# Attention: weights times v in six products of 256 columns per block instead of four of 512, and some subtractions moved from VectorE to GpSimd

## The chip, the cores and the metric

The kernel runs on one core of one Trainium2 chip. The metric is device time in microseconds. Before the change three runs gave 906.5, 906.73 and 907.61 us; the median is 906.73. A profile of one further execution (907.17 us) is used for all readings. The engines are named as in the profile: PE is TensorE (PEld its weight loads), DVE is VectorE, ACT is ScalarE, POOL is GpSimd, SP is SyncE, which only issues transfers.

## The reference

One layer of a hybrid block for 1024 tokens of width 1024: a modulated RMSNorm, one input projection, two branches (sliding-window attention and a recurrent branch), their output projections, a merge, an output product, the residual and a last norm. What matters here is the attention:

```python
WINDOW = 128
BLOCK = 128
...
kb = jnp.concatenate([kp[:, :-1], kp[:, 1:]], axis=2)
vb = jnp.concatenate([vp[:, :-1], vp[:, 1:]], axis=2)
s = jnp.einsum('bnqkgd,bnskd->bnkgqs', qb, kb) * (1.0 / math.sqrt(hd))
...
band = (diff >= 0) & (diff < WINDOW)
s = jnp.where(mask[None, :, None, None], s, -1e30)
m = jnp.maximum(jnp.max(s, axis=-1, keepdims=True), sink)
p = jnp.exp(s - m)
denom = jnp.sum(p, axis=-1, keepdims=True) + jnp.exp(sink - m)
o = jnp.einsum('bnkgqs,bnskd->bnqkgd', p / denom, vb)
```

There are 16 query heads in four groups that share a key and value head (head width 64), and 8 blocks of 128 queries. As window and block are both 128, a query sees exactly 128 keys: those of its own block up to itself, and those of the block before that come after its own place. The recurrent branch ends in `y_rnn @ w_rnn_proj`, a full product of 1024 x 1024 by 1024, which also matters below.

## The kernel before, in words

**Precision.** Every product is made of parts: an operand is split into a rounded high part and the rest as a low part (names ending in `h` and `l`), and three of the four products of parts are summed. The high part is a cast on ACT (`cast`, line 105), the low part a subtraction on DVE (`rest`, line 111).

**Stages.** The input projection (line 709) runs to about 557 us, then the attention stage to about 735 us, then the attention's projection, the merge and the output product (line 1863). From the input projection to the end of the attention, the order of each engine's instructions is the order in which the program writes them; a scheduler orders the last stage.

**The attention stage.** It is a loop of 35 iterations over 32 units u: unit u is group g = u // 8 and block n = u % 8, with four heads. It is pipelined: iteration u makes the scores of unit u (line 1330, eight products of 256 columns; `s_ps`), the exponentials of unit u - 1 (ACT, line 1355), the transposed weights of unit u - 2 (line 1369, `pt`) and the product with v of unit u - 3 (line 1403, `pv`). To keep TensorE busy, one or two pieces of *filler* stand between them (`piece`): slots of the input projection that were kept back, then pieces of the recurrent branch's output product (line 173, names `yh`, `yl`, `wh`, `wl`, output `rp`), twelve products of 512 columns each. On TensorE an iteration reads: transposes of u - 2, product of u - 3, scores of u + 1, filler.

**What a unit's scores go through.** ACT copies the scores of the own block (line 1339), DVE puts those of the block before in the places k > q (line 1345, `copy_predicated`, the last reader of `s_ps`, of which there is one buffer), takes the maximum (1350), ACT the exponential, DVE the reciprocal of the sum (1361) and the division (1362). So the 128 weights of a query lie in one row of 128 places k, own block for k <= q, block before for k > q.

**The product with v.** TensorE transposes the four heads' weights into `pt` (keys down, 4 x 128 queries across). ACT rounds it to `phc` (1374), DVE takes the rest, `plc` (1380), and GpSimd makes two masked copies, `phm` and `plm`, in which places k > q are zero (`masks`, line 1389). With v of the block before as if all places were its own, and the difference of the two blocks' v for the masked places, the output is

```python
prods = [(vd[:, n % 2, 1 if n else 0, :], m) for m in full]
prods += [(vd[:, n % 2, 0, :], m) for m in masked]
```

four products of 512 columns, into one PSUM tile `pv`. The stationary side holds v's high part in 64 columns and its low part in the other 64, so each product gives both. ACT and DVE join the two halves (1412, 1413, 1423, 1424) into `yq`. A block with n = 0 has no block before: two products, no masks.

**vd.** `v_prep` (line 1154 on) makes v and its differences for each group early in the program and stores them with two transfers to `vd_d` in DRAM, on GpSimd's queue. `load_v` (1305) loads 256 KB for two neighbouring units, on the same queue, two iterations ahead. The loads of keys and queries, of the recurrent weights (`r`) and of the recurrent branch's outputs (`yh`, `yl`, `load_y`) go through SP's queue. `load_y` is called at the first recurrent pieces, and each `yh` or `yl` of 512 KB is read by the products of its eighth kc.

**Around it.** The gate of the attention is applied in every second iteration by DVE (1538, both operands in SBUF), then ACT rounds (1543) and DVE subtracts (1548, both operands in SBUF) in the next. The filler's weights are split by `prep_r`: the cast is put off to the end of an iteration (`later_a`), the subtraction on DVE to the next iteration, behind the maximum (`later_d`). Two of four recurrent pieces bring one such pair each.

**GpSimd in an iteration:** a copy of the sinks into the place of the 129th weight (1318), the two masks, every second iteration the load of vd.

Of the kernel before, what the change touches and what calls it, by code (L numbers as in the profile page):

```python
# [50 lines left out]
BANKS = (0, 1, 2, 3), (4, 5, 6, 7)  # L51


@with_exitstack
def tile_hybrid_block(ctx, tc, x, pk, rows, posr, posi, c_row, w_ss, w_gate, w_main, w_v,
# [53 lines left out]
    def rest(dst, src, scale=1.0):  # L109
        if scale == 1.0:  # L110
            V.tensor_tensor(out=dst[1][:], in0=src, in1=f32(dst[0][:]), op=ALU.subtract)  # L111
# [18 lines left out]
    vd_d = [tc.dram_tile([P, 8, 2, P], F32, name=f"vd_d{g}") for g in range(NG)]  # L130
# [1023 lines left out]
    def v_prep(g):  # L1154
# [19 lines left out]
        def f3():  # L1174
# [3 lines left out]
            dma(vd_d[g][:, 1:8, 1, :], t["vs"][:, 0:7, :], G)  # L1178
            dma(vd_d[g][:, :, 0, :], t["dv"][:], G)
# [102 lines left out]
    def open_attn():  # L1282
# [9 lines left out]
        load_v(0)  # L1292

# [11 lines left out]
    def load_v(m):  # L1305
        g, n0 = m // 4, (m % 4) * 2
        vd = at.tile([P, 2, 2, P], F32R, tag="vd", name="vd", bufs=2)
        if n0:
            dma(vd[:], vd_d[g][:, n0:n0 + 2, :, :], G)
        else:  # L1310
            dma(vd[:, 0, 0, :], vd_d[g][:, 0, 0, :], G)
            dma(vd[:, 1, :, :], vd_d[g][:, 1, :, :], G)
        U["v", m] = vd
# [51 lines left out]
    def transposed(u):  # L1365
        px = U.pop(("s", u))[1]
        pt = psx.tile([P, 4, P], F32, tag="t", name="pt")
        for j in range(4):
            W["pe"] = T.transpose(pt[:, j, :], px[:, j, 0:P], ident[:])  # L1369
        U["t", u] = [pt]  # L1370

    def split_a(u):
        phc = at.tile([P, 4, P], F32R, tag="phc", name="phc")
        A.copy(phc[:], U["t", u][0][:])
        U["t", u].append(phc)

    def split_d(u):
        pt, phc = U.pop(("t", u))
        plc = at.tile([P, 4, P], F32R, tag="plc", name="plc")
        V.tensor_tensor(out=plc[:], in0=pt[:], in1=f32(phc[:]), op=ALU.subtract)  # L1380
        U["m", u] = phc, plc

    def masks(u):
        phc, plc = U["m", u]
        ms = []
        if u % 8:
            for s_, tag in ((phc, "phm"), (plc, "plm")):
                d_ = W["yo"].tile([P, 4, P], F32R, tag=tag, name=tag)
                G.affine_select(out=d_[:], in_=f32(s_[:]), pattern=[[0, 4], [1, P]],
                                compare_op=ALU.is_ge, fill=0.0, base=0,  # L1390
                                channel_multiplier=-1)
                ms.append(d_)
        U["m", u] = [phc, plc], ms

    def values(u):
        n = u % 8
        vd = U["v", u // 2]
        full, masked = U.pop(("m", u))
        prods = [(vd[:, n % 2, 1 if n else 0, :], m) for m in full]
        prods += [(vd[:, n % 2, 0, :], m) for m in masked]  # L1400
        pv = psx.tile([P, 4 * P], F32, tag="v", name="pv")
        for i, (b, m) in enumerate(prods):
            W["pe"] = T.matmul(pv[:], b, m[:].rearrange("p j q -> p (j q)"),  # L1403
                               start=(i == 0), stop=(i == len(prods) - 1))
        U["pv", u] = [pv[:].rearrange("p (a e q) -> p a e q", a=2, e=2)]
        if n % 2 == 0 and u // 2 + 1 < 16:
            load_v(u // 2 + 1)

    def join_a(u):
        pvv = U["pv", u][0]  # L1410
        ob = W["yo"].tile([P, 2, P], F32, tag="ob", name="ob")
        A.copy(ob[0:64], pvv[64:128, :, 0, :])
        A.copy(ob[64:128], pvv[0:64, :, 1, :])
        U["pv", u].append(ob)

    def join_d(u):
# [5 lines left out]
        yo = W["yq"][:, :, (n % 2) * P:(n % 2 + 1) * P]  # L1422
        V.tensor_tensor(out=yo[0:64], in0=pvv[0:64, :, 0, :], in1=ob[0:64], op=ALU.add)
        V.tensor_tensor(out=yo[64:128], in0=pvv[64:128, :, 1, :], in1=ob[64:128], op=ALU.add)
# [12 lines left out]
    def prep_r(e, i):  # L1437
# [4 lines left out]
        later_d.append(lambda: rest(O[e, i], R[e][i]))  # L1442
# [617 lines left out]
```

## Time and profile before

| | |
|---|---|
| median of three runs | 906.73 us (906.5 to 907.61) |
| profiled execution | 907.17 us, of it 905.5 us span from the first to the last instruction |
| TensorE busy | 895.4 us, 99% of the span, clock 0.999 of full speed |
| VectorE, ScalarE, GpSimd busy | 717.1, 567.4, 124.7 us |
| DMA | 180.74 MB, 200 GB/s over the span |

Lines of the profile give an engine, an operation, what it writes and reads, its shape, a count and a duration. The duration of a product is modelled and overlaps with the next one's, so the distance between starts is what a product costs TensorE. "idle before <-X" is time in which the engine waited for X. For a transfer the profile gives the issue, and the time from there to its landing.

### The profile page before, as it was taken

How to read it: one execution, taken by the hardware profiler on the slowest of the kernel's cores; microseconds unless marked ns; L12 is line 12 of the kernel's file. 1: busy time of each engine (PE TensorE's matmuls, PEld its weight loads, DVE VectorE, ACT ScalarE, POOL GpSimd, SP SyncE). 2: the span in 40 equal slices, each digit the busy share in tenths (PEclk: the TensorE clock that was granted, in tenths of full speed). 3: DMA queues.
4: the chain of work that ended last, by engine and by line, in shares of the span. 5: the costliest groups of instructions: out<-in, count | busy, mean ns of one | idle time of the engine just before them, and what ended most of it. 6: DMA issues, size and time to landing. Idle time of an engine off the chain costs nothing.

```text
span 905.5 us, 12654 instructions
## 1 busy us (share of the span) xinstructions
PE 895.4 (99%) x4258; PEld 746.2 (82%) x4259; DVE 717.1 (79%) x1073; ACT 567.4 (63%) x1098; POOL 124.7 (14%) x216
## 2 busy tenths in 40 slices
PE   9999999999999999999999999999999999999997
PEld 6789888888888888888888888888888888888886
DVE  6987688988669875987788597999989846578855
ACT  7965554654566855786485884888888732115535
POOL 6520251200000000000000002343443300000000
PEclk9999999999999999999999999999999999999999
DMA  9829489772435353354446367996655289416604
GB/s 355 339 69 286 164 258 319 256 235 95 151 128 180 123 209 135 125 183 162 157 144 213 105 201 242 344 401 217 214 202 203 83 306 367 140 47 232 209 1 186
DMA packets 87349, 180.74 MB, mean 200 GB/s; under 512 B 8642, under 2 KB 29138, under 8 KB 87284
## 3 DMA queue, kind: packets, MB, share of 16 engines
q1 hardware_dynamic: 83200, 167.07, 52.5%
q0 software_dynamic: 3936, 12.59, 4.4%
q8 instruction: 34, 0.56, 0.3%
q14 instruction: 31, 0.25, 0.1%
q10 hardware_dynamic: 148, 0.27, 0.1%
HBM read 121.34 MB, written 58.95 MB: 199 GB/s over the span
## 4 chain that ended last, share of the span: by engine, by line
PE 52%; issue 42%; DVE 3%; ACT 2%; DMA 1%; POOL 0%; DVEq 0%; ACTq 0%; POOLq 0%
PE rp L173 14%; PE bk L709 10%; PE out L1863 6%; PE pmain L173 5%; PE s_ps L1330 3%; PE pv L1403 3%; PE pmain L485 2%; PE bk L485 2%; PE pt L1369 1%; DMA yl_d<-it 1%; PE pmain L1579 1%; PE pmain L1580 1%; PE pmain L1578 1%; ACT jk L1881 1%; PE bk L256 1%
## 5 line engine op out<-in xcount | busy, mean ns | idle before, releaser
L709 PE MATMUL bk<-nh,wh 128*128 128x512 f32 x368 | 143.4, 390 | 0.0
L709 PE MATMUL bk<-nl,wh 128*128 128x512 f32 x368 | 143.3, 389 | 0.0
L709 PE MATMUL bk<-nh,wl 128*128 128x512 f32 x368 | 98.4, 389 | 0.0
L111 DVE TENSOR_TENSOR wl<-r,wh 128x512 fp32r<-128x512 f32 x109 | 74.8, 692 | 23.3 <-ACT wh L105 23.2
L105 ACT CAST wh<-r 128x512 fp32r<-128x512 f32 x107 | 65.6, 618 | 32.1 <-PE rp L173 11.8
L709 PEld LDWEIGHTS bk<-nh,wl 128*128 128x128 f32 x368 | 69.1, 188 | 14.3
L709 PEld LDWEIGHTS bk<-nh,wh 128*128 128x128 f32 x368 | 69.2, 188 | 14.2
L709 PEld LDWEIGHTS bk<-nl,wh 128*128 128x128 f32 x368 | 69.1, 188 | 14.1
L709 PE MATMUL bk<-hh,wh 128*128 128x512 f32 x184 | 71.7, 390 | 0.0
L709 PE MATMUL bk<-hl,wh 128*128 128x512 f32 x184 | 71.6, 389 | 0.0
L111 DVE TENSOR_TENSOR wl<-ws,wh 128x512 fp32r<-128x512 f32 x76 | 52.1, 686 | 7.2 <-ACT wh L105 7.1
L62 POOL DMA_DIRECT2D yh_d<-av x1 | 0.6, 567 | 371.9 <-ACT av L1092 371.9
L1355 ACT ACTIVATE p<-p,small 128x129 f32<-128x129 f32 x128 | 50.0, 396 | 0.0
L709 PE MATMUL bk<-hh,wl 128*128 128x512 f32 x184 | 49.2, 389 | 0.0
L105 ACT CAST wh<-ws 128x512 fp32r<-128x512 f32 x76 | 46.0, 614 | 4.8 <-DVE ws L731 2.4
L709 PEld LDWEIGHTS bk<-hh,wl 128*128 128x128 f32 x184 | 34.6, 188 | 7.1
L709 PEld LDWEIGHTS bk<-hh,wh 128*128 128x128 f32 x184 | 34.6, 188 | 7.1
L709 PEld LDWEIGHTS bk<-hl,wh 128*128 128x128 f32 x184 | 34.6, 188 | 7.1
L1330 PEld LDWEIGHTS s_ps<-ks,qs 128*128 128x128 f32 x256 | 34.1, 189 | 4.4 <-DVE p L1345 2.0
L1330 PE MATMUL s_ps<-ks,qs 128*128 128x256 f32 (+1 forms) x256 | 35.6, 282 | 0.3 <-DVE p L1345 0.2
L709 PE MATMUL bk<-hha,wh 128*128 128x512 f32 x92 | 35.8, 390 | 0.0
L709 PE MATMUL bk<-hla,wh 128*128 128x512 f32 x92 | 35.8, 389 | 0.0
(378 smaller groups left out, 2293.1 us busy)
## 6 DMA issues: line engine op xcount, KB each, us to landing
r<-w_main SPq DMA_DIRECT2D x100, 256.0 KB, 4.2
wada<-w_ss SPq DMA_DIRECT2D x16, 512.0 KB, 9.0
qs<-q_d SPq DMA_DIRECT2D x16, 512.0 KB, 5.2
wo_d<-wr SPq DMA_DIRECT2D x28, 256.0 KB, 3.1
wo<-wo_d SPq DMA_DIRECT2D x14, 512.0 KB, 5.6
ks<-k_d SPq DMA_DIRECT2D x12, 384.0 KB, 4.3
xt<-x SPq DMA_DIRECT2D x8, 512.0 KB, 7.1
sma_d<-c SPq DMA_DIRECT2D x16, 256.0 KB, 4.4
```

The source lines that it names most:

```text
L105: A.copy(dst[0][:], src)
L111: V.tensor_tensor(out=dst[1][:], in0=src, in1=f32(dst[0][:]), op=ALU.subtract)
L173: mm = T.matmul(ps[hf], ww, xx[kc][hf], start=(kc == 0 and ww is w_h and xx is xh), stop=(kc == KC - 1 and xx is xl))
L256: T.matmul(bk[i % 2], zero[:, 0:P], zero, start=True, stop=True)
L485: T.matmul(starts[c][hf], ww[:, c0:c0 + P], xh[kc][hf], start=(kc == 0 and t_ == "h"), stop=(kc == KC - 1 and t_ == "l"))
L709: W["pe"] = T.matmul(ps, ww[:, kc * P:(kc + 1) * P], b[kc][i], start=(first and n == 0), stop=(n == 11), skip_group_check=not first)
L1330: W["pe"] = T.matmul(o, qs[:, j, qc], ks[:, kb:n % 2 + 2, b, :], start=(b == 0), stop=(b == 1))
L1355: A.activation(px[:, j, :], px[:, j, :], AF.Exp, bias=sm[:, 0, j:j + 1], accum_out=sm[:, 1, j:j + 1])
L1369: W["pe"] = T.transpose(pt[:, j, :], px[:, j, 0:P], ident[:])
L1403: W["pe"] = T.matmul(pv[:], b, m[:].rearrange("p j q -> p (j q)"), start=(i == 0), stop=(i == len(prods) - 1))
L1578: T.matmul(o, hh[kc][th][:, ts_], wh[:, cols], start=(kc == 0), stop=False)
L1863: T.matmul(o, a[k][x_][:, p * P:(p + 1) * P], b[k][y_][:, cols], start=(first and k == 0 and i == 0), stop=(k == 3 and i == 2), skip_group ...
```

## The change

The columns of the product with v are regrouped: the 128 queries of a block are taken in two halves l of 64, so that 4 heads x 64 queries make 256 columns. For the lower half, places 64 to 127 always belong to the block before, so only places 0 to 63 need the mask; for the upper half places 0 to 63 always belong to the own block, and only 64 to 127 need it. So the masked high and the masked low part of a half each fill only 64 partitions, and both go into one tile `pm` of 128 partitions, against a stationary side that holds the difference twice. Each half has three products of 256 columns (`phc`, `plc`, `pm`). `vd` now holds, for each unit and each half, its own base and its own doubled difference.

What goes with it:
- `v_prep` stores eight transfers for each group instead of two, and `vd_d` is twice as large.
- `load_v` loads 256 KB for each unit instead of for two (64 KB where n = 0), with three buffers.
- The transposes write two pieces of 64 columns; the joins read four-dimensional views.
- `masks` makes four selects of 64 x 256 instead of two of 128 x 512; two of them read one half of the partitions and write the other.
- In the attention stage the filler's low parts are subtracted by GpSimd, at the end of the iteration, right behind the cast; VectorE has 18 subtractions fewer.

The diff's core:

```diff
-    def rest(dst, src, scale=1.0):
+    def rest(dst, src, scale=1.0, eng=V):
         if scale == 1.0:
-            V.tensor_tensor(out=dst[1][:], in0=src, in1=f32(dst[0][:]), op=ALU.subtract)
+            eng.tensor_tensor(out=dst[1][:], in0=src, in1=f32(dst[0][:]), op=ALU.subtract)
...
-            dma(vd_d[g][:, 1:8, 1, :], t["vs"][:, 0:7, :], G)
-            dma(vd_d[g][:, :, 0, :], t["dv"][:], G)
+            o, vs, dv = vd_d[g], t["vs"], t["dv"]
+            dma(o[:, 1:8, 0, 0, :], vs[:, 0:7, :], G)
+            dma(o[:, 0, 0, 0, :], vs[:, 0, :], G)
+            dma(o[TOP, 1:8, 1, 0, :], vs[TOP, 1:8, :], G)
+            dma(o[END, 1:8, 1, 0, :], vs[END, 0:7, :], G)
+            for l, half_ in enumerate((TOP, END)):
+                for to in (TOP, END):
+                    dma(o[to, 1:8, l, 1, :], dv[half_, 1:8, :], G)
...
-    def load_v(m):
-        g, n0 = m // 4, (m % 4) * 2
-        vd = at.tile([P, 2, 2, P], F32R, tag="vd", name="vd", bufs=2)
-        if n0:
-            dma(vd[:], vd_d[g][:, n0:n0 + 2, :, :], G)
+    def load_v(u):
+        g, n = u // 8, u % 8
+        vd = U["v", u] = at.tile([P, 2, 2, P], F32R, tag="vd", name="vd", bufs=3)
+        if n:
+            dma(vd[:], vd_d[g][:, n, :, :, :], G)
...
-            for s_, tag in ((phc, "phm"), (plc, "plm")):
-                d_ = W["yo"].tile([P, 4, P], F32R, tag=tag, name=tag)
-                G.affine_select(out=d_[:], in_=f32(s_[:]), pattern=[[0, 4], [1, P]],
+            pm = W["yo"].tile([P, HALF], F32R, tag="pm", name="pm")
+            lo, hi = slice(0, 256), slice(256, HALF)
+            for to, s_, from_, cols in ((TOP, phc, TOP, lo), (END, phc, END, hi),
+                                        (END, plc, TOP, lo), (TOP, plc, END, hi)):
+                G.affine_select(out=pm[to, cols], in_=f32(s_[from_, cols]),
+                                pattern=[[0, 4], [1, 64]], compare_op=ALU.is_ge, fill=0.0,
...
-        for i, (b, m) in enumerate(prods):
-            W["pe"] = T.matmul(pv[:], b, m[:].rearrange("p j q -> p (j q)"),
-                               start=(i == 0), stop=(i == len(prods) - 1))
-        if n % 2 == 0 and u // 2 + 1 < 16:
-            load_v(u // 2 + 1)
+        for l in range(2 if n else 1):
+            cols = slice(l * 256, l * 256 + 256) if n else slice(0, HALF)
+            for i, t_ in enumerate(m):
+                W["pe"] = T.matmul(pv[:, cols], vd[:, l, i // 2, :], t_[:, cols],
+                                   start=(i == 0), stop=(i == len(m) - 1))
+        if u + 2 < 32:
+            load_v(u + 2)
...
-        later_d.append(lambda: rest(O[e, i], R[e][i]))
+        later_d.append(lambda: rest(O[e, i], R[e][i], eng=G if "att" in W else V))
...
-        do_later(later_d)
         low = [steps_[2] for steps_ in high]
...
-        do_later(later_a)
+        do_later()
```

How the instructions stand now. TensorE, the transposes of one unit, the product with v of the unit before and the scores that follow; before:

```order
L1369 MATMUL pt<-ident,p 128x128 x4
L1403 MATMUL pv<-phc,vd 128x512
L1403 MATMUL pv<-plc,vd 128x512
L1403 MATMUL pv<-phm,vd 128x512
L1403 MATMUL pv<-plm,vd 128x512
L1330 MATMUL s_ps<-ks,qs 128x256 x8
```

The same place on TensorE now:

```order
L1375 MATMUL pt<-ident,p 128x2x64 x4
L1409 MATMUL pv<-phc,vd 128x256
L1409 MATMUL pv<-plc,vd 128x256
L1409 MATMUL pv<-pm,vd 128x256
L1409 MATMUL pv<-phc,vd 128x256
L1409 MATMUL pv<-plc,vd 128x256
L1409 MATMUL pv<-pm,vd 128x256
L1336 MATMUL s_ps<-ks,qs 128x256 x8
```

Four products became six of half the width; nothing else on TensorE changed its place in the whole program.

GpSimd, two iterations near unit 6, before (the sinks' copy, the masks, the select of a first block's scores, loads of vd):

```order
L62 DMA vd<-vd_d_85 128x512
L1318 COPY p<-pk_t 128x4
L1389 AFFINE_SELECT phm<-phc 128x512
L1389 AFFINE_SELECT plm<-plc 128x512
L1348 AFFINE_SELECT p<-p 128x4x128
L1318 COPY p<-pk_t 128x4
L1389 AFFINE_SELECT phm<-phc 128x512
L1389 AFFINE_SELECT plm<-plc 128x512
L62 DMA vd<-vd_d_86 128x128
```

The same two iterations on GpSimd now:

```order
L63 DMA vd<-vd_d_85 128x512
L1324 COPY p<-pk_t 128x4
L1396 AFFINE_SELECT pm<-phc 64x256 x2
L1396 AFFINE_SELECT pm<-plc 64x256 x2
L112 TENSOR_TENSOR wl<-r,wh 128x512
L1354 AFFINE_SELECT p<-p 128x4x128
L63 DMA vd<-vd_d_85 128x512
L1324 COPY p<-pk_t 128x4
L1396 AFFINE_SELECT pm<-phc 64x256 x2
L1396 AFFINE_SELECT pm<-plc 64x256 x2
L112 TENSOR_TENSOR wl<-r,wh 128x512
L63 DMA vd<-vd_d_86 128x128
```

The subtraction stands behind the masks and ahead of the next load of vd, and there is a load in each iteration. VectorE at the same place, one iteration before:

```order
L1548 TENSOR_TENSOR al<-yq,ah 128x2x256
L1345 COPY_PREDICATED p<-mgt,s_ps 128x4x128
L1350 TENSOR_REDUCE small<-p 128x4
L111 TENSOR_TENSOR wl<-r,wh 128x512
L1361 RECIPROCAL small<-small 128x4
L1362 TENSOR_TENSOR p<-p,small 128x4x128
```

and now:

```order
L1554 TENSOR_TENSOR al<-yq,ah 128x2x256
L1351 COPY_PREDICATED p<-mgt,s_ps 128x4x128
L1356 TENSOR_REDUCE small<-p 128x4
L1367 RECIPROCAL small<-small 128x4
L1368 TENSOR_TENSOR p<-p,small 128x4x128
```

Only the subtraction left; line 1548 (1554 now) keeps its place ahead of line 1345 (1351), and a subtraction on GpSimd falls in that stretch of the iteration. In the last stage, which the scheduler orders, a few loads on SP and a few casts and subtractions on ACT and DVE change places among themselves.

More of the change, by code (lines that the diff above doesn't have):

```diff
@@ L1378, in split_d @@
         pt, phc = U.pop(("t", u))
[L1379 to L1380 removed]
+        plc = at.tile([P, HALF], F32R, tag="plc", name="plc")
+        V.tensor_tensor(out=plc[:], in0=pt, in1=f32(phc[:]), op=ALU.subtract)
         U["m", u] = phc, plc
```

45 lines of the change are left out of this document (20 added, 25 removed).

## The prediction

> **What bounds the kernel now.** I read the page's shares first, then the table of stretches (engine busy time, granted clock, DMA share), then the timelines of the attention stage, and last who waited for whom.
>
> ```profile
> PE 895.4 (99%) x4258; PEld 746.2 (82%) x4259; DVE 717.1 (79%) x1073; ACT 567.4 (63%) x1098; POOL 124.7 (14%) x216
> ...
> 570.00:616.50 46.50, 46.41 (x261) 39.56 (x260) 43.27 (x79) 39.17 (x124) 19.13 (x36) 1.00 1.01 381
> 616.50:735.00 118.50, 118.50 (x637) 100.64 (x636) 103.89 (x195) 93.66 (x289) 42.33 (x74) 1.00 0.52 178
> 735.00:905.50 170.50, 163.99 (x735) 136.02 (x733) 111.45 (x155) 61.97 (x109) 0.00 (x0) 0.99 0.50 184
> ```
>
> The columns after a stretch are its length, then PE, PEld, DVE, ACT and POOL busy, the clock, the DMA share and GB/s. TensorE is busy throughout and at full clock, so a microsecond taken off its stream is a microsecond off the end, as long as nothing else becomes late. The attention stage (about 557 to 735 us) is where something can: VectorE is busy 93% in the first of its two stretches, and there the DMA engines are full, with a share of 1.01 at 381 GB/s. From 616.5 us on the DMAs have half of their time free.
>
> **The change part by part.** *The products.* One iteration of the attention loop on TensorE, up to the next one's transposes, then two neighbours of the 256-column products that make v, which load new weights for each product, and the count of the masked products:
>
> ```profile
> 644.08 0.60 PE L1369 MATMUL pt<-ident,p 128*128 128x128 f32 x4
> 644.44 0.48 PE L1403 MATMUL pv<-phc,vd 128*128 128x512 f32 x1
> 644.75 0.39 PE L1403 MATMUL pv<-plc,vd 128*128 128x512 f32 x1
> 644.99 0.40 PE L1403 MATMUL pv<-phm,vd 128*128 128x512 f32 x1
> 645.22 0.39 PE L1403 MATMUL pv<-plm,vd 128*128 128x512 f32 x1
> 645.45 1.11 PE L1330 MATMUL s_ps<-ks,qs 128*128 128x256 f32 x8
> 646.40 0.40 PE L173 MATMUL rp<-hha,wh 128*128 128x512 f32 x1
> ...
> 649.15 0.60 PE L1369 MATMUL pt<-ident,p 128*128 128x128 f32 x4
> ...
> 75.00 0.28 PE L1578 MATMUL pmain<-wh,hha 128*128 128x256 f32 x1
> 75.12 0.28 PE L1579 MATMUL pmain<-wl,hha 128*128 128x256 f32 x1
> ...
> L1403 PE MATMUL pv<-phm,vd x28: 389/397/398, 579.0 to 729.5; 128*128 128x512 f32 x28
> ```
>
> Only starts count here, as the shown durations overlap. The four products hold TensorE from 644.44 to 645.45, 1.01 us: 0.31 to the second start and 0.23 for each of the others, so the first one, behind the transposes, costs 0.08 extra. A 256-column product costs 0.12 us (75.00 to 75.12; the eight of the scores take 0.95, 0.119 each). Six make 6 x 0.12 + 0.08 = 0.80 us. The saving is 0.21 us in each of 28 blocks (the four with n = 0 keep two products of 512): 5.9 us. Taken with 0.119 and no weight load showing it is 0.22, or 6.2 us. I take 28 x 0.215 = 6.0 us. The four transposes stay four of 128 columns, written as two pieces of 64, and the joins of line 1412 to 1424 move the same number of elements; I cost both at nothing. If a piece cost 10 ns more, the joins would still be hidden behind TensorE's filler, and the 128 transposes would cost 1.3 us.
>
> *Loads of vd.* This is the term against the change. Before, one load of 256 KB serves two blocks; now each block with n > 0 loads its own 256 KB, 64 KB for n = 0. The stretch in which this happens is the one with full DMA engines, and it holds the loads of the recurrent branch's y, which the filler products read:
>
> ```profile
> vd<-vd_d POOLq DMA_DIRECT2D x4, 256.0 KB, 6.4
> vd<-vd_d POOLq DMA_DIRECT2D x1, 128.0 KB, 5.3
> vd<-vd_d POOLq DMA_DIRECT2D x1, 64.0 KB, 5.2
> ...
> 606.58 0.32 SPq L62 DMA_DIRECT2D yl<-yl_d  x1
> ...
> yl<-yl_d SPq DMA_DIRECT2D x1, 512.0 KB, 9.9
> ...
> 618.04 0.62 PE L173 MATMUL rp<-yl,wh 128*128 128x512 f32 x2
> ...
> 585.00:590.00 5.00, 5.00 (x30) 4.28 (x29) 4.20 (x8) 4.43 (x15) 2.25 (x5) 1.00 0.95 310
> ```
>
> The last y piece was issued at 606.58 and landed 9.9 us later, at 616.5; its first reader starts at 618.04. That is 1.5 us of slack. The vd loads of 570 to 616 move 4 x 256 + 128 + 64 = 1216 KB before. Afterwards about eight of 256 and one of 64 fall there, 2112 KB: 0.9 MB more, at 381 GB/s 2.4 us of all engines. From 585 to 590 the engines had a share of 0.95, so 0.25 us is free there; and about half of the last load, 0.35 us, comes too late to matter. I take 1.7 us: the piece lands at 618.2. Its reader would be ready at 618.04 less the seven shortened blocks u = 1 to 7 (1.5 us), at 616.5, so TensorE waits 1.7 us there and is then 0.2 us behind the old time. The 21 blocks after it save 21 x 0.215 = 4.5 us. Bounds: no wait at all (6.0 us kept) and the whole 2.4 us (3.7 us kept).
>
> The stores that prepare vd_d go from two to eight on GpSimd's queue for each of four groups. They stand ahead of the next group's load of v there, but that load is asked for six slots ahead and TensorE reads vd_d only in the attention stage; I cost them at nothing. If that cover failed, VectorE would wait some microseconds for v in a stage in which TensorE has its weights in hand.
>
> *GpSimd.* It loses two selects of 128x512 per block and gets four of 64x256, and it gets 18 of VectorE's subtractions. Durations that stand nearest:
>
> ```profile
> L1389 POOL TENSOR_SCALAR_AFFINE_SELECT plm<-plc 128x512 fp32r<-128x512 f32 x28 | 17.7, 632 | 15.0 <-DVE plc L1380 14.4 <-PE s_ps L1330 0.6
> masks.py:199 POOL TENSOR_SCALAR_AFFINE_SELECT ident<-ident 128x128 f32<-128x128 f32 x1 | 0.3, 287 | 0.1
> L62 POOL DMA_DIRECT2D vd<-vd_d x20 | 11.0, 553 | 2.3 <-PE pv L1403 2.0 <-issue 0.3
> 120.45 0.20 POOL L1140 TENSOR_TENSOR lam_p<-lam_p,lam_s 128x8 f32<-128x8 f32 x1
> L297 POOL TENSOR_TENSOR a<-ang,t 128x64 f32<-128x64 f32 x1 | 0.3, 320 | 0.1
> L351 POOL TENSOR_TENSOR trn<-trn,r 128x128 f32<-128x128 f32 x1 | 0.6, 578 | 0.1
> ```
>
> From 287 ns at 128 columns and 632 at 512 a select of 256 takes 0.40 us, four take 1.6. No row shows a select that moves data between partition halves; between 0.29 and 0.63 each, I take 0.40. A subtraction of 128x512: from 0.20 at 8 columns and 0.32 at 64 it is 0.32 + 448 x 2.1 ns = 1.3 us; by the step from 64 to 128 (0.26 us) it would be 2.1; a one-input pass of this size took 0.63. I take 1.2. [...] With a vd load (0.55) and a sink copy (0.2) an iteration with a subtraction asks 3.6 us of GpSimd, of an iteration of 5.07 (644.08 to 649.15) less 0.21 = 4.86 us, so it is not the bound.
>
> *VectorE* loses 18 x 0.69 = 12.4 us, all beside TensorE's work, so worth nothing by itself. What it gets is a neighbour:
>
> ```profile
> L111 DVE TENSOR_TENSOR wl<-r,wh 128x512 fp32r<-128x512 f32 x109 | 74.8, 692 | 23.3 <-ACT wh L105 23.2
> ...
> 636.15 0.68 DVE L1380 TENSOR_TENSOR plc<-pt,phc 128x512 fp32r<-128x512 f32 x1
> 637.17 0.43 DVE L1424 TENSOR_TENSOR yq<-pv,ob 64x256 f32<-64x256 f32 x1
> ...
> 636.97 0.63 POOL L1389 TENSOR_SCALAR_AFFINE_SELECT plm<-plc 128x512 fp32r<-128x512 f32 x1 [0.24 <-DVE plc L1380]
> 637.56 0.64 POOL L1348 TENSOR_SCALAR_AFFINE_SELECT p<-p 128x512 f32<-128x512 f32 x1
> 637.63 1.11 DVE L1538 TENSOR_TENSOR yq<-yq,r 128x512 f32<-128x512 f32 x1
> ```
>
> GpSimd's select began at 637.56; VectorE's product of two SBUF operands began 0.07 us later and took 1.11 us instead of 0.69: it stood until the select was done. [...] GpSimd's subtraction comes right behind the selects on plc, just where VectorE comes to line 1538 or 1548 (one of the two stands there in each iteration). By the rows: plc ends at 636.83, the first select on it starts 0.14 later, and two selects of 0.36 to 0.40 end 0.86 to 0.94 behind plc; VectorE is at line 1538 by 637.60, 0.77 behind plc. [...] When VectorE comes second it loses up to 1.2 us, and behind it stand line 1345, which frees the bank of the scores, and TensorE's next scores:
>
> ```profile
> 624.35 0.74 DVE L1345 COPY_PREDICATED p<-mgt,s_ps 128x512 f32<-128x512 uint32 x1
> ...
> 624.78 0.40 PE L1403 MATMUL pv<-plm,vd 128*128 128x512 f32 x1
> 625.14 0.62 PE L1330 MATMUL s_ps<-ks,qs 128*128 128x256 f32 x3
> ```
>
> Here that wait shows already: the scores start 0.36 behind the last product instead of 0.23, 0.05 after line 1345 ended. Usually there is about 1 us of room. I allow 0.5 us for lost races and take 0.3 off for such small waits as this, which a freer VectorE no longer causes: 0.2 us net, bounds -0.3 and +7 (the loss, below).
>
> *The sum.* The profiled execution took 907.17 us, 905.5 of it span; the median of the runs shown is 906.73, 0.44 lower. Waiting 0.2 us behind at the y load, then -4.5, then +0.2: -4.1 us, so 903.1 on the profile's scale and 902.6 on the median's. The stage from 735 us on keeps TensorE's order; a small reshuffle of its loads, casts and subtractions I take as free, since TensorE is busy there for 163.99 of 170.50 us, the end included.
>
> **The rivals.** *The y loads come in time* (0.2). Against it speaks the full share of 1.01, for it that the loads are asked for earlier when TensorE is earlier. Then 6.0 less 0.2 is kept: 906.7 - 5.8 = 900.9 us.
>
> *GpSimd's subtraction wins the race each time* (0.1): the loss. It decides when the subtraction takes 1.2 us or more and starts first in both of the two neighbouring iterations out of four that hold one. One iteration of VectorE that holds no subtraction, from reciprocal to reciprocal:
>
> ```profile
> 625.80 0.17 DVE L1361 RECIPROCAL small<-small 128x4 f32<-128x4 f32 x1
> ...
> 630.26 0.17 DVE L1361 RECIPROCAL small<-small 128x4 f32<-128x4 f32 x1
> ```
>
> It takes 4.46 us of the 4.86, so four iterations have 4 x 0.4 = 1.6 us to spare. Two blocks of 1.25 us ask 2.5: 0.9 us over in each of some eight rounds, 7 us of waiting at the scores. Then 902.6 + 7 = 909.6 us. [...] For it: VectorE is late already in some iterations; against it: the tenth of a microsecond above. Where only one of the two races is lost (0.13), 1.25 of 1.6 us is eaten, most waits stay small, and with some 3 us lost the time is 905.6, no change or little gain.
>
> *The products do not get cheaper* (0.05): weight loads of 0.19 us each that no longer hide behind 0.12 us of columns would make six cost 1.2 us. The v products speak against it, at 0.12 with a new load each. Then the y load costs nothing, as TensorE is late anyway: 906.7 + 28 x 0.2 = 912 us.
>
> **How the numbers follow.** The forecast with its bounds holds 0.52, the others as said. I count what moves by less than 0.2%, 1.8 us, as no change, which is about what a measurement of this kernel can tell. Faster: 0.52 + 0.2 and about 0.07 of the half-lost races, 0.79. Same: the rest of those and the edges, 0.09. Slower: 0.12. The range leaves out the two slower cases above and the last corner below: 900.3 to 905.6.
>
> **What would show it.** Right: products of pv starting 0.12 apart and blocks of 0.80 us; one wait of one to two microseconds of TensorE for the y load near 616 us; line 1538 or 1548 stretched in a few iterations only; subtractions of about 1.2 us on GpSimd. Wrong: blocks over 0.95 us; no wait near 616 us (then the time is near 901); waits of the scores for line 1345 in most rounds, or of pv for the selects, which would put the time above 905.

## The result and the profile after

The changed kernel takes 916.16 us (median of 4 runs, 915.66 to 917.44) where the kernel before takes 906.89 us beside it (4 runs, 906.50 to 907.61): a ratio of 1.0103, with a 95% interval of 1.0086 to 1.0121. It is 9.3 us slower; 4.1 us faster were forecast. In a second comparison, below, it is 12.8 us slower (919.76 against 906.97). The profiled execution has a span of 913.9 us, against 905.5.

From the page of the changed kernel, the engines' shares, the granted clock by fortieths of the span, and GpSimd's DMA queue (packets, MB, share of the 16 DMA engines):

```profile
PE 896.0 (98%) x4314; PEld 748.8 (82%) x4315; DVE 710.1 (78%) x1055; ACT 567.1 (62%) x1098; POOL 177.5 (19%) x326
PEclk9999999799999999999999999999999999999999
q0 software_dynamic: 6496, 19.94, 7.5%
```

The clock's line has one 7, in the eighth slice (160 to 183 us), far ahead of the attention. In the kernel before, the same queue has this row:

```profile
q0 software_dynamic: 3936, 12.59, 4.4%
```

It moves 7.35 MB more now, for 3.1% of the span of all engines, some 28 us. The waits of TensorE in the changed kernel (in all, how often, the longest) begin with two that the kernel before does not have:

```profile
PE bk L710 <- DVE wl L114: 5.3, 1, 5.3
PE bk L710 <- ACT wh L108: 2.9, 1, 2.9
```

Where they lie shows a table of stretches, first of the kernel before, then of the changed one (columns as in the prediction):

```profile
140.00:150.00 10.00, 10.00 (x46) 8.29 (x45) 8.31 (x12) 4.75 (x9) 1.00 (x2) 1.00 0.97 324
150.00:160.00 10.00, 10.00 (x46) 8.29 (x45) 7.70 (x11) 4.14 (x8) 0.00 (x0) 1.00 0.91 308
160.00:170.00 10.00, 10.00 (x45) 8.27 (x45) 9.67 (x16) 6.33 (x12) 2.86 (x4) 1.00 0.70 225
```

```profile
150.00:160.00 10.00, 6.62 (x30) 5.14 (x28) 1.00 (x2) 1.95 (x4) 0.00 (x0) 1.00 1.00 284
160.00:170.00 10.00, 8.12 (x26) 6.49 (x27) 7.55 (x11) 3.67 (x7) 0.00 (x0) 0.66 0.66 235
170.00:180.00 10.00, 7.11 (x32) 5.57 (x31) 7.35 (x12) 3.65 (x8) 6.91 (x10) 1.00 0.97 260
180.00:190.00 10.00, 10.00 (x39) 8.08 (x38) 8.78 (x16) 6.34 (x13) 0.00 (x0) 0.83 0.81 258
```

TensorE loses 8.15 us there by waiting, and more by the clock, which stands at 0.66 and 0.83 behind the two waits. How much in all is read from the first scores of the attention and the first filler product behind its last product, in the timeline before and after:

```profile
557.84 1.00 PE L1330 MATMUL s_ps<-ks,qs 128*128 128x128 f32 x8
...
729.91 0.61 PE L173 MATMUL rp<-yh,wh 128*128 128x512 f32 x2
```

```profile
570.77 1.00 PE L1336 MATMUL s_ps<-ks,qs 128*128 128x128 f32 x8
...
738.47 0.63 PE L174 MATMUL rp<-yh,wh 128*128 128x512 f32 x2
```

The attention begins 12.9 us late. It then lasts 167.7 us, not 172.1: there the change gains 4.4 us. What follows is as long as before to 0.2 us (913.9 - 738.5 = 175.4, and 905.5 - 729.9 = 175.6). So 12.9 lost - 4.4 gained = 8.5 us, for the 8.4 us between the spans. Of the 12.9, 0.3 are there at 30 us already, ahead of the first store: from 24.7 to 26.9 us products of 512 columns start 0.43 us apart in this execution, 0.23 in that of the kernel before, and the distance of 0.3 stays until 155 us. All the rest falls where the operands vd_d are stored (lines 1179 to 1186) and the output gate's weights are loaded, 360 us and more before the attention reads what was stored.

How the loss comes about stands in the timeline of the changed kernel: VectorE's gate sums, ScalarE's ones, GpSimd's stores and memset, TensorE:

```profile
147.36 0.54 SPq L63 DMA_DIRECT2D wr<-w_gate  x1
159.93 1.29 DVE L1212 SCALAR_TENSOR_TENSOR gate_bc<-wr,pk_t,gate_bc 128x1024 f32<-128x1024 f32 x1 [9.00 <-DMA wr<-w_gate]
161.13 0.69 DVE L114 SCALAR_TENSOR_TENSOR wl<-ws,wh 128x512 fp32r<-128x512 f32 x1
161.88 2.08 PE L710 MATMUL bk<-nh,wl 128*128 128x512 f32 x4 [5.26 <-DVE wl L114]
...
173.27 2.89 POOL L63 DMA_DIRECT2D vd_d<-dv  x4
176.97 0.23 POOL L1220 MEMSET wr<- 128x128 f32 x1
177.23 0.30 ACT L1222 CAST ones_r<-wr 128x128 fp32r<-128x128 f32 x1 [6.32 <-POOL wr L1220]
179.15 0.50 PE L710 MATMUL bk<-nh,wh 128*128 128x512 f32 x1 [2.89 <-ACT wh L108]
```

A load of the gate's weights, issued at 147.36, is waited for until 159.93. On VectorE the low part that TensorE needs (line 114) stands behind the gate's sum and starts at 161.13. The longest time from issue to landing of these wr loads, before and after (shortest, median, longest):

```profile
DMA to landing us min/median/max: 4.1/4.8/5.2
```

```profile
DMA to landing us min/median/max: 3.9/4.8/12.5
```

Later the memset stands in GpSimd's order behind a group's eight stores, which take GpSimd 5.9 us to issue (1.9 us for the two before). ScalarE's cast of the ones waits 6.3 us for it (2.2 before), and TensorE's next weights stand behind that on ScalarE. What the engines of the DMA do meanwhile, in a view of 10 us around a group's stores, first before (138 to 148 us), then after (140 to 150 us):

```profile
DMA packets 1777, 3.27 MB, mean 327 GB/s; under 512 B 161, under 2 KB 1080, under 8 KB 1777
...
vd_d<-dv POOLq DMA_DIRECT2D x1, 512.0 KB, 7.7
sma_d<-c SPq DMA_DIRECT2D x2, 256.0 KB, 5.8
```

```profile
DMA packets 1580, 2.82 MB, mean 282 GB/s; under 512 B 158, under 2 KB 1005, under 8 KB 1579
...
vd_d<-dv POOLq DMA_DIRECT2D x4, 224.0 KB, 12.0
sma_d<-c SPq DMA_DIRECT2D x2, 256.0 KB, 13.5
```

Four stores of 64 partitions have taken the place of the one of dv with 128, and three more stand beside the one of vs. SyncE's stores of sma_d, which have nothing to do with the change, land 7.7 us later (13.5 against 5.8), while the engines, busy for a share of 0.92 of this window against 1.00, move 282 GB/s instead of 327.

### The profile page after: what moved, and what is told of

Its sections match the earlier page's. It is cut to its first block, busy times and chain, and to the rows that moved or that the text cites. A ratio compares the mean times of both kernels' runs of the same rounds, so it can differ in the third digit from the quotient of the medians.

```text
span 913.9 us, 12880 instructions
## 1 busy us (share of the span) xinstructions
PE 896.0 (98%) x4314; PEld 748.8 (82%) x4315; DVE 710.1 (78%) x1055; ACT 567.1 (62%) x1098; POOL 177.5 (19%) x326
## 4 chain that ended last, share of the span: by engine, by line
PE 48%; issue 42%; DVE 3%; DMA 2%; ACT 2%; POOL 2%; SPq 0%; DVEq 0%; ACTq 0%; POOLq 0%
PE rp L174 13%; PE bk L710 9%; PE out L1868 6%; PE pmain L174 5%; PE s_ps L1336 3%; PE bk L486 3%; PE pmain L486 2%; PE pv L1409 2%; PE pt L1375 1%; POOL vd_d L63 1%; PE pmain L1586 1%; PE pmain L1585 1%; PE pmain L1584 1%; DMA yl_d<-it 1%; DMA wr<-w_gate 1%
## 5 line engine op out<-in xcount | busy, mean ns | idle before, releaser
L112 DVE TENSOR_TENSOR wl<-r,wh 128x512 fp32r<-128x512 f32 x91 | 62.0, 689 | 20.6 <-ACT wh L106 19.3
L710 PE MATMUL bk<-hh,wl 128*128 128x512 f32 x184 | 49.2, 389 | 0.0
```

Of the source, the lines that this page charges most:

```text
L112: eng.tensor_tensor(out=dst[1][:], in0=src, in1=f32(dst[0][:]), op=ALU.subtract)
L710: W["pe"] = T.matmul(ps, ww[:, kc * P:(kc + 1) * P], b[kc][i], start=(first and n == 0), stop=(n == 11), skip_group_check=not first)
```

## The experiments

Theory A: the six further stores of each group, at the place where they stand, cost the 12.9 us; the attention's own gain is 4.4 us. Rivals: the loss comes from another part of the change; or from the bytes, wherever they move; or from GpSimd's queue alone. Each diff stands against the changed kernel where nothing else is said.

**The stores of before.** The operands are not doubled; a load reads each row twice, so the output is not that of the reference.

```
-            dma(o[:, 1:8, 0, 0, :], vs[:, 0:7, :], G)
-            dma(o[:, 0, 0, 0, :], vs[:, 0, :], G)
...
+            dma(o[:, 1:8, 1, :], vs[:, 0:7, :], G)
+            dma(o[:, :, 0, :], dv[:], G)
...
-            dma(vd[:], vd_d[g][:, n, :, :, :], G)
+            dma(vd[:], vd_d[g][:, n:n + 1, :, :].to_broadcast([P, 2, 2, P]), G)
```

> The changed kernel with the stores of before (two for each of the four groups, 4.7 MB on GpSimd's queue over the run instead of 8.4 MB of stores). The duplicated rows are left out: each load reads the old rows twice, so the output is not the reference's; every instruction of the attention stays. Theory A (the 12.9 us lost before the attention come from the six further stores of each group, and the attention itself gains 4.4 us): the attention begins at 557.8 us again, TensorE has no wait over 1 us between 120 and 200 us, and the time is 906.9 - 4.4 = 902.5 us (901.5 to 904). Rival B (the loss comes from the rest of the change, the larger loads or GpSimd's subtractions): 912 to 916 us.

Measured: 903.73 us, ratio 0.9966 (0.9953 to 0.9979). The attention begins at 557.71 us and lasts 168.3, and TensorE waits for nothing between 120 and 200 us. Theory A holds; the rest of the change loses nothing outside the attention. The time is 1.2 us above the forecast: of the attention 0.6 us are missing against the 167.7 above, and a wait at its start accounts for 0.4 of them (0.67 us for ScalarE's p, against 0.25; below).

**The stores alone, without the change.** Against the kernel before; six stores for each group, of the shapes that the change has. They add 1024 KB to a group's stores, the change 896 KB.

```
+            o, vs, dv, lo, hi = vx_d[g], t["vs"], t["dv"], slice(0, 64), slice(64, 128)
+            dma(o[:, 0, 0, :], vs[:, 0, :], G)
+            dma(o[lo, 1:8, 0, :], vs[lo, 1:8, :], G)
+            dma(o[hi, 1:8, 0, :], vs[hi, 0:7, :], G)
...
```

> The kernel before, with six further stores for each group of heads, of the same shapes and at the same place as in the change, into DRAM that nothing reads. Theory A: the whole loss without the gain, 906.9 + 12.9 = 919.8 us (917 to 922), TensorE waiting for VectorE's low parts and for ScalarE's casts between 155 and 185 us. Rival B: 906.5 to 908 us.

Measured: 922.87 us (918.70 to 924.92), ratio 1.0171 (1.0149 to 1.0193). Its two waits of TensorE:

```profile
PE bk L710 <- DVE wl L113: 5.2, 1, 5.2
PE bk L710 <- ACT wh L107: 2.7, 1, 2.7
```

They are those of the changed kernel, with no change in the attention. The time is 0.9 us above the expected range. The loss is 16.2 us in the medians and 11.7 in the profiled execution (the attention begins at 569.58), which is the shortest of the four. Theory A holds for the cause; the size scatters, and whether the 128 KB more of a group add to it is not shown.

**The copies later, on GpSimd.** About as many bytes as before are stored at the old place (the first four lines, instead of the eight stores), the rest is copied from DRAM to DRAM, five copies for each group.

```
             dma(o[:, 1:8, 0, 0, :], vs[:, 0:7, :], G)
...
+            dma(o[TOP, 1:8, 0, 1, :], dv[TOP, 1:8, :], G)
+            dma(o[END, 1:8, 1, 1, :], dv[END, 1:8, :], G)
+            dma(o[TOP, 7, 1, 0, :], vs[TOP, 7, :], G)
+            copies = ((o[:, 0, 0, 0, :], o[:, 1, 0, 0, :]),
+                      (o[TOP, 1:7, 1, 0, :], o[TOP, 2:8, 0, 0, :]),
...
+                at_slot(70 + 20 * g + 4 * i,
+                        ("N", 0, 0, lambda to=to, from_=from_: dma(to, from_, G)))
```

> The changed kernel, complete, but the six further stores of each group are taken out of the place where the weights of the output gate are loaded: GpSimd stores four pieces there (as many bytes as before), and five copies from DRAM to DRAM for each group fill the rest some 80 to 250 us later, where the trace of the changed kernel shows the DMA engines busy for 0.40 to 0.48 and GpSimd idle. Theory A: it is the place and not the bytes that cost; the attention begins at 558 us, 902.5 us in all (901.5 to 904), faster than the kernel before. Rival C (any further 3.7 MB cost, wherever they are moved): some stall of TensorE between 270 and 460 us and a time between 905 and 914 us.

Measured: 906.33 us, ratio 0.9992 (0.9983 to 1.0001): the loss is gone, and most of the gain too. The timeline of GpSimd in this kernel shows that the copies did not go where the slots put them:

```profile
181.65 3.44 POOL L63 DMA_DIRECT2D vd_d<-vd_d  x5
...
188.40 6.78 POOL L63 DMA_DIRECT2D vd_d<-vd_d  x10 [1.95 <-DMA vd_d<-dv]
```

A slot sets a place in an engine's order, and GpSimd, with nothing else in its order, was there at once: all twenty were issued between 182 and 201 us. The DMA engines stood at 0.97 from 175 to 200 us, and TensorE lost 0.45 us in two waits between 200 and 220. The attention begins at 559.68 us in the profile, 1.8 late. Of that, 0.75 us are there at 30 us already, ahead of any store; the clock stands at 0.91 and 0.75 there (20 to 25 and 25 to 30 us; 1.00 in the kernel before). The other 1.1 arise at 195 to 215 us, and the two waits make up 0.45 of them. The time misses Theory A's range and lies in Rival C's, but the copies did not run where either expected them, from 270 to 460 us, so this run does not decide between them. A plan must give the DMA a neighbour that waits.

**The same, with the subtractions on VectorE.** To the copies on GpSimd: the filler's subtractions at their place of before.

```
-        later_d.append(lambda: rest(O[e, i], R[e][i], eng=G if "att" in W else V))
+        later_d.append(lambda: rest(O[e, i], R[e][i], eng=V))
...
+        do_later(later_d)
         low = [steps_[2] for steps_ in high]
...
-        do_later()
+        do_later(later_a)
```

> The kernel of the DRAM copies, with the 18 subtractions of the filler's weight pieces back on VectorE and at their old place. Theory A: the six narrower products alone carry the gain of 4.4 us, so that it stays within 1 us of the kernel of the DRAM copies (902 to 903.5 us). Rival D (GpSimd's subtractions carry a part, because VectorE is the engine that the attention's small waits name): 904 to 906.5 us. Rival E (GpSimd's 1.48 us subtraction is a cost, against 0.69 us on VectorE): under 901.5 us.

Measured: 906.21 us, ratio 0.9988 (0.9980 to 0.9997), beside 906.33. The engine of the subtractions makes no difference that these medians show (0.1 us); the level missed its range (902 to 903.5) with its partner's, for the reason above.

**The copies on SyncE.** Against the copies on GpSimd.

```
-                        ("N", 0, 0, lambda to=to, from_=from_: dma(to, from_, G)))
+                        ("N", 0, 0, lambda to=to, from_=from_: dma(to, from_)))
```

> The kernel of the DRAM copies, with the copies issued by SyncE instead of GpSimd. In the first try GpSimd had nothing else to do and issued all twenty at 182 to 201 us, where the DMA engines then stood at 0.97 to 1.03; in SyncE's queue they stand between loads and stores that wait for their own tiles, and so come apart in time, between 270 and 460 us by their places in the order. Theory A (place, not bytes): no wait of TensorE between 180 and 220 us, the attention begins at 557.8 us, and the time is that of the two stores, 903.7 us, give or take 1. Rival C (the bytes cost wherever they are): 906 us or more, with waits of TensorE between 270 and 460 us.

Measured: 904.30 us, ratio 0.9968 (0.9956 to 0.9981). The attention begins at 557.67 us. The twenty copies are issued from 293 to 533 us now, where the DMA engines' share is 0.47 to 0.55, and TensorE waits for nothing there. At this share the bytes cost nothing; Rival C falls. What is left is the wait at the attention's start:

```profile
PE s_ps L1341 <- ACT p L1350: 1.3, 1, 1.3
```

**The tiles p moved.** Against the copies on SyncE.

```
+        W["pp"] = pool(at_ctx, "pp", bufs=3, side="right")
+        W["pp"].tile([P, 72], F32, name="pad", bufs=1)
         W["yo"] = pool(at_ctx, "yo", side="right")
-        W["pp"] = pool(at_ctx, "pp", bufs=3, side="right")
-        W["pp"].tile([P, 72], F32, name="pad", bufs=1)
```

> The same, and the pool of the tiles p is opened ahead of the pool yo, so that the first p no longer lies where the last yl is stored from (in the changed kernel ScalarE's first copy into p waits 5.3 to 5.9 us for that store, and TensorE 0.25 to 1.6 us behind it; in the kernel before, TensorE had no such wait). Theory A: 0.7 us less than the kernel with the copies on SyncE, and no wait of s_ps for ScalarE's p: 902.5 to 903.5 us. Rival F (the wait only moves to the next tile that lies there): the same time as without it, within 0.4 us.

Measured: 902.55 us (902.24 to 903.46), ratio 0.9950 (0.9937 to 0.9964), the fastest of all. Two tiles of masked weights became one, which moved the pool behind them; that put the first p on the memory from which the recurrent branch's last part is stored. The wait is gone and the time is 1.75 us shorter, where 0.7 was expected; Rival F falls. Of this kernel the stretch in which the changed one lost most:

```profile
150.00:160.00 10.00, 10.00 (x46) 8.28 (x45) 5.86 (x8) 3.52 (x7) 0.00 (x0) 1.00 0.81 281
```

The attention begins at 558.12 us and lasts 167.4.

**The same with the subtractions on VectorE.** The edit of the fourth experiment.

> The kernel with the copies on SyncE and p moved, with the 18 subtractions of the filler's weight pieces on VectorE again. By the earlier pair (906.33 and 906.21 us) the engine of these subtractions makes no difference: within 0.5 us of the kernel with p moved. If GpSimd's subtractions help once the other losses are gone: 1 to 2 us more.

Measured: 903.69 us (902.16 to 904.01), ratio 0.9956 (0.9944 to 0.9969). That is 1.1 us above its partner, more than the 0.5 expected, with ranges that overlap. The attention lasts 167.4 us here too; what the two profiles differ by lies ahead of it (559.46 against 558.12 us), where the subtractions are the same: 0.7 us in the first 30 us of the kernel, ahead of any store, and 0.6 between 150 and 175 us. So in the attention of these two profiles GpSimd's subtraction is neither a cost nor a gain.

**The memset on VectorE.**

```
-            G.memset(o[:, 0:P], 1.0)
+            V.memset(o[:, 0:P], 1.0)
```

> The changed kernel, with one instruction moved: the 128x128 memset of wr behind the stores in GpSimd's queue is made by VectorE. It tells apart the two parts of the loss of 12.9 us. If the stores cost by GpSimd's queue (ScalarE's ones_r waits for the memset, TensorE 2.9 us for ScalarE's weights, and half clock for some microseconds after it) and by the full DMA engines (5.3 us and half clock after it), only the first goes: 916.2 - 2.9 - 1.7 = 911.6 us (910.5 to 913). If the queue is the whole cause: 903 to 905 us. If the memset only happens to stand there: 916 us.

Measured: 914.17 us, ratio 1.0078 (1.0064 to 1.0092), between two of the expected times. The wait for ScalarE is gone, but the one for VectorE is as long as both were, 8.2 us, though nothing ahead of it had moved. So the changed kernel and this one were run again, side by side:

> The changed kernel once more, unchanged, as the partner of the next run on the same chip: 916 us, TensorE's two waits again, for VectorE (5.3 us in the first profile) and for ScalarE (2.9 us). What it is to show is how far the first of them scatters from one execution to the next: if it is 4 to 9 us here, the 8.2 us of the kernel with the memset on VectorE are scatter of the loads; if it is 5 to 5.5 again, they are not.

> The changed kernel with the memset of wr on VectorE, once more. If the first wait of 8.2 us was scatter: 5 to 6 us of waiting for VectorE and none for ScalarE, and 3 to 4.6 us less than the changed kernel beside it. If the loss of the second wait is given back at the first: 8 us again, and 2 us less than the changed kernel, as in the first comparison.

Measured: 919.76 us for the changed kernel (919.27 to 921.34; ratio 1.0141, 1.0124 to 1.0158) and 916.70 for the one with the memset moved (912.71 to 918.07; 1.0095, 1.0070 to 1.0120). TensorE's waits in the profile of each:

```profile
PE bk L710 <- DVE wl L114: 6.3, 1, 6.3
PE bk L710 <- DVE wl L112: 2.7, 1, 2.7
```

```profile
PE bk L710 <- DVE wl L114: 6.4, 1, 6.4
PE bk L710 <- ACT wh L108: 1.6, 1, 1.6
```

So the first wait scatters, from 5.2 to 8.2 us in the five profiles with all stores at the old place, and a wait for ScalarE comes without the memset on GpSimd too. (The changed kernel has one of 1.0 us here, behind the two shown.) The 2.7 us are a wait that its first profile does not have. VectorE stands until 141.7 us for a group's v, and the low part that TensorE needs next stands behind that:

```profile
DVE d L1165 <- DMA v<-v_d: 6.4, 1, 6.4
```

This load is issued behind a group's eight stores on GpSimd's queue. With the lower clock after it (0.93 on average from 125 to 150 us), it costs TensorE 4.5 us in this execution.

The memset behind the stores carries 2 to 3 us of the loss by the two pairs of medians (2.0 and 3.1), where the times of one kernel lie up to 5.4 us apart; how much exactly stays open. The wait for v is a second cost on that queue, in one profile of five. The longest wait is not on it: SyncE issues the loads of wr, and their late landing is in every one of these profiles.

**Half the dose.** The products' full rows are stored at the old place, only the differences' second rows are copied later by SyncE. The tiles p are moved as above.

```
-            for l, half_ in enumerate((TOP, END)):
-                for to in (TOP, END):
-                    dma(o[to, 1:8, l, 1, :], dv[half_, 1:8, :], G)
+            dma(o[TOP, 1:8, 0, 1, :], dv[TOP, 1:8, :], G)
+            dma(o[END, 1:8, 1, 1, :], dv[END, 1:8, :], G)
+            copies = ((o[END, 1:8, 0, 1, :], o[TOP, 1:8, 0, 1, :]),
+                      (o[TOP, 1:8, 1, 1, :], o[END, 1:8, 1, 1, :]))
...
```

> Half the dose: the kernel with the copies on SyncE and p moved, but the products' full rows are stored directly, all of them, by GpSimd at their old place, and only the doubled rows of the differences are copied later (5.8 MB stored there, against 3.8 MB with all copies later and 7.6 MB in the changed kernel). Theory A, with the DMA engines as a queue that is served in proportion: VectorE's wait for the gate's weights halfway between 2.8 and 9.0 us, 5.9 us; 3.7 us of that were covered in the changed kernel (9.0 of VectorE against 5.3 of TensorE), so TensorE waits some 2 us and loses one more by the clock: 905.5 us (903.5 to 908). If there is a threshold that half the dose doesn't reach: 902.5 to 903.5 us. If the number of stores counts and not the bytes (six of the eight are there): 908 us or more.

Measured: 907.95 us (906.57 to 910.98), ratio 1.0010 (0.9999 to 1.0022), at the edge between two of the expectations. VectorE's longest wait with all copies later (the kernel with p moved), then VectorE's and TensorE's waits with half of them:

```profile
DVE gate_bc L1217 <- DMA wr<-w_gate: 4.2, 2, 2.8
```

```profile
DVE gate_bc L1216 <- DMA wr<-w_gate: 7.0, 2, 5.3
```

```profile
PE bk L710 <- DVE wl L114: 1.8, 2, 1.2
PE bk L710 <- ACT wh L108: 1.4, 1, 1.4
```

VectorE's longest wait is 5.3 us (5.9 expected), between 2.8 with all copies later and 9.0 in the changed kernel, and TensorE waits 3.2 us: the loss grows with what is stored there, and part of it is there at half the dose. Six stores of a group instead of eight, with half of the further bytes, cost 4.5 to 5.4 us against the two times of the kernel with p moved; whether number or bytes count is not told apart. The clock stayed at 1.00 in the profiled execution, which is among the shorter ones (906.83 us).

**Once more.** The kernel with p moved, in another comparison.

> The kernel with the copies on SyncE and p moved, once more, since the changed kernel's loss came out 3.6 us apart in its two comparisons (916.2 and 919.8 us). Theory A: the loss scatters because it hangs on when loads land among full DMA engines; without it nothing of that size is left to scatter, so that this kernel comes out within 1.5 us of its first time, 902.6 us, 4 to 5 us below the kernel before. If it scatters as far as the changed kernel did, something else is shared by both.

Measured: 903.45 us (902.55 to 904.93), ratio 0.9961 (0.9947 to 0.9974), 0.9 us from its first time, within the 1.5 expected, and 3.5 below the kernel before (4 to 5 expected). The changed kernel's two medians lie 3.6 us apart. That its loss scatters because it hangs on landings fits this, but two comparisons of each do not show it: within one, this kernel's times range over up to 2.4 us, the changed kernel's over up to 2.1.

## Why the prediction was wrong

**The step that failed** is the price of the stores: "The stores that prepare vd_d go from two to eight on GpSimd's queue for each of four groups. [...] I cost them at nothing. If that cover failed, VectorE would wait some microseconds for v in a stage in which TensorE has its weights in hand." Two things in it were wrong. I looked for who waits for what these stores write and for who stands behind them in their queue, and found only v. But the transfers share 16 DMA engines with all others (in the kernel before, from 138 to 148 us, GpSimd's queue takes 38.8% of them and q1, the largest queue, 61.2%), and the table of stretches of the kernel before gives these a share of 0.97 and 0.91 from 140 to 160 us: next to no room. I read that share for the vd loads, 400 us later, and not for the stores. And "TensorE has its weights in hand" took no account of VectorE's order: one late load of the gate holds the low parts of TensorE's weights that stand behind it. Nor did I list the memset behind the stores in GpSimd's queue. The one case that the passage names, v coming late, did occur in the changed kernel's second profile (VectorE 6.4 us, TensorE 2.7 behind it), and TensorE did not have its weights in hand there either. The runs with only the stores added, or only the stores undone, put the loss on them: 16.2 us lost by the medians of the one, and 903.73 us in the other.

The shape of these stores I had not weighed either. Four stores of 224 KB from 64 partitions land 12.0 us behind their issue (the median) where one of 512 KB from 128 took 7.7. All transfers of that window together move 282 GB/s instead of 327, a seventh less, at an engine share of 0.92 instead of 1.00; no run separates the shape from the bytes.

**The products** were right. One block of the changed kernel's timeline, to compare with the prediction's:

```profile
640.58 0.60 PE L1375 MATMUL pt<-ident,p 128*128 128x128 f32 x4
640.93 0.36 PE L1409 MATMUL pv<-phc,vd 128*128 128x256 f32 x1
641.13 0.28 PE L1409 MATMUL pv<-plc,vd 128*128 128x256 f32 x1
...
641.73 1.12 PE L1336 MATMUL s_ps<-ks,qs 128*128 128x256 f32 x8
```

Six products hold TensorE from 640.93 to 641.73, 0.80 us as forecast, 0.12 apart. Added up by their starts, the 28 masked blocks take 22.7 us, before 28.6: 5.9 us saved, 6.0 forecast. The blocks with n = 0 gave 0.55 back (0.73 instead of 0.54 for three of the four), which I had not seen; with the subtractions on VectorE they take 0.54 to 0.55, but others grow, and the attention is as long.

**The y loads** cost nothing, where I had taken 1.7 us. The rival of loads in time was right in its outcome. In the changed kernel, the last y piece, how long the six take to land, and the reader of that piece:

```profile
L63 SPq DMA_DIRECT2D yl<-yl_d x6: 320/418/672, 595.0 to 620.0; - x6
...
DMA to landing us min/median/max: 8.1/9.2/11.9
```

```profile
630.41 0.62 PE L174 MATMUL rp<-yl,wh 128*128 128x512 f32 x2
```

Issued at 620.0, it lands by the median at 629.2, and its reader comes at 630.41. Counted from the attention's start, the reader comes 0.6 us earlier than before and not 1.5, and the landing is no slower (9.2 us, 9.9 before). The rival's ground is not what is seen: the load is issued 49.2 us behind that start, 48.7 before, so not earlier.

**The small waits** cost more than forecast. I allowed a net cost of 0.2 us; of 5.9 saved, less the 0.55 at n = 0, 4.4 are left, so they took 0.95. Of that, 0.25 us (0.2 to 1.6 in the experiments that leave p there) fall at the attention's start, where the moved tile p waits for a store. I had not read the memory's layout, in which the change takes out one tile and adds one elsewhere. **GpSimd's** instructions, in the changed kernel:

```profile
L1396 POOL TENSOR_SCALAR_AFFINE_SELECT pm<-phc 64x256 fp32r<-64x256 f32 x56 | 28.0, 500 | 21.9 <-ACT phc L1380 19.9
L112 POOL TENSOR_TENSOR wl<-r,wh 128x512 fp32r<-128x512 f32 x18 | 26.6, 1480 | 10.6 <-ACT wh L106 9.0 <-POOL pm L1396 0.6
L1396 POOL TENSOR_SCALAR_AFFINE_SELECT pm<-plc 64x256 fp32r<-64x256 f32 x56 | 23.5, 419 | 6.1 <-DVE plc L1386 1.7 <-ACT rp L1490 1.2
```

A select takes 0.42 to 0.50 us (0.40 forecast), a subtraction 1.48 (1.2). The race with VectorE's two-operand products is seen (line 1554 takes 949 ns on average; 727 before, as line 1548, and 734 with the subtractions on VectorE and p moved) and costs nothing that the comparison of the two engines shows. For the order I had a tenth of a microsecond, VectorE at 0.77 us behind plc and GpSimd, by an estimate of its selects, at 0.86; in the changed kernel both orders occur. At 624.94 us line 1554 takes 1.30 us (0.70 is the shortest), beside a subtraction that GpSimd began at 624.39; at 644.35 the subtraction takes 1.61 us (1.28 is the shortest), beside a line 1554 that began at 644.04. The price of a race was my estimate, with one row behind it in which a product took 0.42 us longer: no run shows the 0.5 us that I allowed for lost races, nor the 7 us of the loss, and with the subtractions on one engine or the other the medians are 906.33 and 906.21 us. So the sum for the attention, -4.1, was near -4.4 partly by luck, as 1.7 us too much for the y loads stood against 1.3 us too little for the blocks with n = 0 and the small waits. The sum for the program left out 12.9.

## What to carry to other kernels

A transfer that nobody waits for can still have a price (most of 12.9 us here): look up the DMA share at its own place and time, and follow who is late when every other load there lands later, through the order of each engine's instructions down to the bound one. Data that is needed late can be completed late, if the copy is issued from a queue that waits with the work (904.30 us with the copies on SyncE, against 916.16); a place in the order of an idle engine is no time (906.33 us with them on GpSimd). And taking out or adding a tile can move the others (a wait of 0.2 to 1.6 us here): read what the first user of each moved buffer waits for.

## What the hardware showed besides

The longer waits of TensorE cost more than their length here. Behind the 5.26 us, matmuls of 512 columns start 0.43 us apart for nearly five microseconds, instead of 0.23 as in the lines of the prediction:

```profile
163.75 0.63 PE L710 MATMUL bk<-hh,wh 128*128 128x512 f32 x1
164.17 0.63 PE L710 MATMUL bk<-hl,wh 128*128 128x512 f32 x1
```

From 161.88 to 166.73 that is some 2.3 us lost (4.85 x (1 - 0.227/0.425)), and behind the wait of 2.89 us about 1.6 more, from 180.43 to 183.84. Together with the two waits it makes 12.0 of the 12.9 us; 0.3 lie at the start of the kernel, and 0.6 are not assigned. Behind the wait of 2.7 us for v in the second profile, four products take 2.07 us, where four take 1.07 at the full clock. The waits of at most 1.45 us in the half dose left the clock at 1.00. Behind the 2.89 us the slow stretch begins 1.3 us after TensorE had begun again (180.43 against 179.15). The granted clock is 0.50 in both stretches of the first profile.
